# Hybrid decoder step: first output tile and weight splits one or two steps later in the last stage, and the sample's result stored by two transfers

## The chip, the cores and the metric

The kernel runs on one core of a Trainium2 chip. The metric is the device time of one execution in microseconds. Times of engines, waits and transfers come from one profiled execution, whose own clock starts at its first instruction.

## What is computed

One layer of a hybrid trunk, for a prompt of 1024 positions and for 64 sample positions (8 sequences of 8). What the last stage does of it, cut from the reference:

```python
# sample: selected-block attention over a cache of 8192 positions per sequence
s = jnp.einsum('bthgd,bhtkd->bhgtk', q, kb) * SCALE
p = masked_softmax(s, (kpos <= tq[None, None, :, None])[:, :, None])
return jnp.einsum('bhgtk,bhtkd->bthgd', p.astype(vb.dtype), vb)

# prompt and sample: output projection, residual, final norm
def merge(a, z_a, b, z_b, w_out):
    return jnp.concatenate([a * jax.nn.silu(z_a), b * jax.nn.silu(z_b)], axis=-1) @ w_out

x_p = x_p + merge(a_out, z_a, b_out, z_b, w_out[l])   # (1, 1024, 1024)
x_s = x_s + merge(a_out, z_a, b_out, z_b, w_out[l])   # (8, 8, 1024)
return (rmsnorm(x_p, final_g), rmsnorm(x_s, final_g), ...)
```

Arithmetic is float32. The output projection is made of three products of rounded halves: high by high, high by low, low by high.

## The kernel before

Earlier stages do the projections, the prompt's attention and the sample's compressed branch. The last stage, which the change touches, has 64 steps. A step is one piece of the cache (512 positions) of two sequences:

- `load(p_, e)` (line 1590) fetches the step's eight blocks of 128 KB into two `kv` tiles. Most are direct transfers that SP issues, each after a page number that SP loads from `pgt`; the others are gathers that GpSimd (POOL) issues. Up to step 4 one block of eight is a gather, from step 5 on three are. There are twelve `kv` tiles, six steps' worth, so the load of step i+6 needs the tiles of step i, which are free after `o` of step i.
- `step_k` (line 1726) transposes the keys on TensorE (`pk`, eight matmuls), and ACT copies them out (`kt`).
- `step_a` (line 1618) makes the scores (`pss`) and DVE adds the mask and takes the maxima (`Sx`, `st`); `exps` (line 1632) is ACT's exponential over `Sx`, one step later.
- `step_b` (line 1636) transposes the probabilities (`pp` on TensorE, `pT` on ACT); `step_c` (line 1639) multiplies them with the values (`o`), two steps after the scores.

Between these stand the output projection's products (`yacc`): `OutTile` (line 1469) loads a tile of 128 prompt rows (`mt`, one buffer, two transfers), `high` rounds it on ACT (`mh`), `low` makes the remainder on DVE (`ml`), `product` multiplies with the high and low part of `w_out` (`woh`, `wol`). `wo_load` (line 1441) fetches the eight row blocks of `w_out` (`wor`), `wo_split` (line 1451) makes their two parts: the copy is ACT's for odd blocks and DVE's for even ones, the subtraction DVE's. The list `when` gives each product the step from which it is due: the first at step `first`, then evenly up to the last step.

PE, ACT and DVE run in the order in which the loop of line 1745 is written: in step i the exponential of step i-1, the scores of step i, half of the due products around the transposes of step i+1, the transposed probabilities of step i-1, then whatever `at(i, ...)` has listed for this step (tiles' parts first, then weight splits), the other products, and `o` of step i-2. POOL and SP aren't ordered by hand: a scheduler places their transfers. All engines work through their own rows strictly in order.

SP has eight completion semaphores in turn, so that one of its transfers is issued only after the one eight before it has landed.

In the end `SampleTile.finish` (line 1563) normalises the sample's 64 rows, which lie as two halves of 512 columns on 128 partitions (`xf`), and line 1583 stores them. In the names of rows, `kv_9742` and the like are buffer numbers that the build gives; they differ from build to build. SPq is SP's DMA queue, `wor<-in_w_out_dram` a transfer into `wor`.

Of the kernel before, what the change touches and what calls it, by code (L numbers as in the profile page):

```python
# [40 lines left out]
def tok_cols(t):  # L41

    return (0, NS) if t == 0 else (NS + P * (t - 1), P)
# [131 lines left out]
def tile_hymba_gmlp_nsa_decode_step(  # L175
# [9 lines left out]
    V, A, G, TE, SY = (Timed(e, n, clock) for e, n in ((nc.vector, "DVE"), (nc.scalar, "ACT"), (nc.gpsimd, "POOL"),  # L185
                                                       (nc.tensor, "PE"), (nc.sync, "SP")))
# [38 lines left out]
    with ExitStack() as es:  # L225
# [367 lines left out]
        for g_ in ((1, 2, 3, 4, 5, 6, 7, 8), (0,)):  # L593
            for t in g_:
                n = tok_cols(t)[1]
# [12 lines left out]
        for p_ in range(4):  # L608
            for b2 in range(2):
                b = 2 * p_ + b2  # L610
# [110 lines left out]
    with ExitStack() as es:  # L721
# [401 lines left out]
        def prompt_attention():  # L1123
# [197 lines left out]
            for i in range(len(steps) + 1):  # L1321
# [11 lines left out]
                if i >= 2:  # L1333
                    yield done.need_values(1)
                    done.values(1)
                    n_, g_, br_ = steps[i - 2]
                    if g_ in (None, 3):
                        yield [Qs[n_]["o"]] + ([] if g_ is None else [Qs[n_]["x"]]), [] if g_ is None else [tp]
                        collect(Qs[n_], br_)
                    if g_ == 3 and br_ == 1:  # L1340
                        finish(Qs[steps[i - 2][0]])
                        load_z(Qs[steps[i - 2][0] + 1])
# [16 lines left out]
            yield [Qs[7]["o"], Qs[7]["x"]], [tp]  # L1359
            collect(Qs[7], 1)  # L1360
            finish(Qs[7])


# [20 lines left out]
        with tc.manual_schedule(engines={mybir.EngineType.PE, mybir.EngineType.Activation, mybir.EngineType.DVE}):  # L1384
# [5 lines left out]
            while streams or later:  # L1390
# [6 lines left out]
                t = clock.t["PE"]  # L1397
# [8 lines left out]
    with ExitStack() as es:  # L1406
# [27 lines left out]
        def at(step, fn):  # L1434
            todo.setdefault(step, []).append(fn)
# [15 lines left out]
        def wo_split(k):  # L1451
            raw = raws[k]
            if k:
                wol.append(pwo.tile([P, DM], F32R, name="wol", tag="wo", bufs=KC))
            else:
                wol.append(pwo1.tile([P, DM], F32R, name="wol0"))
            (A.copy if k % 2 else V.tensor_copy)(woh[:, k], raw)
            (V if k % 2 else V).tensor_tensor(wol[k], raw, woh[:, k].bitcast(F32), op=ALU.subtract)
# [64 lines left out]
        class SampleTile(OutTile):  # L1523
# [39 lines left out]
            def finish(self):  # L1563
                xt, fg = self.xt, self.fg
                junk = p3b.tile([P, DM], BF16, name="junk", tag="junk", bufs=1)
                ss = p3b.tile([P, 4], F32, name="ss3", tag="ss3")
                rs = p3b.tile([P, 4], F32, name="rs3", tag="ss3")
                for i in range(2):
                    cs = slice(i * 256, i * 256 + 256)
                    V.tensor_tensor(xt[:, cs], xt[:, cs], self.acc[:, cs], op=ALU.add)  # L1570
                    A.activation(junk[:, cs], xt[:, cs], AF.Square, scale=1.0 / 32, accum_out=ss[:, i:i + 1])
                tot = psP.tile([P, 512], F32, name="tot", tag="p")
                for i in range(2):
                    TE.matmul(tot[:, 0:1], both, ss[:, i:i + 1], start=(i == 0), stop=(i == 1))
                G.tensor_tensor(xt, xt, fg, op=ALU.mult)
                V.tensor_scalar(rs[:, 0:1], tot[:, 0:1], EPS, None, op0=ALU.add)
                V.reciprocal(rs[:, 1:2], rs[:, 0:1])
                A.activation(rs[:, 2:3], rs[:, 1:2], AF.Sqrt)

                V.tensor_scalar(rs[:, 1:2], rs[:, 0:1], rs[:, 2:3], rs[:, 2:3], op0=ALU.mult, op1=ALU.mult)  # L1580
                V.tensor_scalar(rs[:, 3:4], rs[:, 1:2], 3.0, rs[:, 2:3], op0=ALU.subtract, op1=ALU.mult)
                V.tensor_scalar(xt, xt, rs[:, 3:4], -0.5, op0=ALU.mult, op1=ALU.mult)
                SY.dma_start(y_sample.rearrange("b t (h c) -> h (b t) c", h=2), xt)


        steps = [(p_, e) for p_ in range(4) for e in range(16)]
# [100 lines left out]
                    V.tensor_tensor(mts[hs, 4:8, ts_], pt_[hs, 0, r_:r_ + 32].rearrange("p (g t) -> p g t", t=TD),  # L1687
                                    zbs[hs, :, ts_], op=ALU.mult)

        n_steps, ahead, first = len(steps), 3, 2  # L1690
        tiles = [OutTile(t) for t in range(1, NT)]
        sample = SampleTile()
        prods = [(o, i) for o in tiles for i in range(6 * KC)]
# [4 lines left out]
        for o, t in zip(tiles, range(len(tiles))):  # L1698
            b0, b1_, b2_ = (when[prods.index((o, i))] for i in (0, 23, 47))
            if t:  # L1700
                at(b0 - 5, o.load)
            at(max(b0 - 3, 0), o.high)
            at(max(b0 - 2, 0), o.low)
            at(b0, o.residual)
            at(b1_ + 1, lambda o=o: o.add(0, o.acc0))
            at(b2_ + 1, lambda o=o: o.add(1, o.acc))
            at(b2_ + 2, o.square)
            at(b2_ + 3, o.root)
            at(b2_ + 4, o.norm)
# [22 lines left out]
        for k in range(KC):  # L1732
            wo_load(k)
        k0 = 0
        for i, n in ((0, 2), (1, 1), (2, 1), (3, 2), (4, 2)):
            for k in range(k0, k0 + n):
                at(i, lambda k=k: wo_split(k))
            k0 += n
# [119 lines left out]
```

## Time and profile before

| | us |
|---|---|
| median of 3 runs (lowest to highest) | 1424.33 (1422.97 to 1429.22) |
| profiled execution, its own time | 1429.88 |
| its span, first to last instruction | 1427.8 |
| the last stage in it, from the first `pk` on | 1061.5 to 1427.8 |

Every row of the profile names an engine, an operation with the tile that it writes and those that it reads, the number of instructions merged into the row, and in brackets the idle time of the engine before it with what ended it. "issue" there is a wait of which the profile shows no cause. The granted clock of TensorE is given as a share of 2.4 GHz (1.00), so 0.50 is 1.2 GHz. The DMA share is the mean of 16 DMA engines, so one engine alone gives 0.06; it can come out a little above 1 when short packets overlap.

### The profile page before, as it was taken

The page shows a single profiled execution, that of the slowest core. Times are in us where ns is not written, and L with a number is a line of the kernel's source. Part 1 is how long each engine was busy: PE and PEld are TensorE (multiplying, and loading weights), DVE is VectorE, ACT ScalarE, POOL GpSimd, SP SyncE. Part 2 cuts the span into 40 slices and gives each one's busy share as a digit, 9 for nine tenths or more (in the row PEclk, how much of TensorE's full clock was granted, in tenths as well). Part 3 has the DMA queues.
Part 4 walks back from the last instruction along what each step waited for, and adds up shares of the span by engine and source line. Part 5 has one row for each costly group of instructions (what it writes and reads, how often), then busy time and mean ns, then how long its engine had stood idle before and what let it go on. Part 6 is the DMA issues. An engine that isn't in the chain of part 4 may idle for free.

```text
span 1427.8 us, 27897 instructions
## 1 busy us (share of the span) xinstructions
PE 1336.1 (94%) x10345; PEld 1044.9 (73%) x10345; DVE 785.2 (55%) x1878; ACT 576.3 (40%) x1275; POOL 568.6 (40%) x684
## 2 busy tenths in 40 slices
PE   6899999999889999999899999999986999999896
PEld 6799999999757776777677776777754666666564
DVE  7527202212487677867678687777765343442334
ACT  5314216421114333354334444263545555555451
POOL 1007426520343363443345343433313566655440
PEclk9999999999999999999999999999998999999998
DMA  7413333535985686665867495663258788787761
GB/s 243 136 36 98 115 80 122 141 65 186 306 298 171 226 302 231 232 207 191 311 223 259 145 320 187 240 224 104 88 183 218 225 254 258 241 249 231 239 193 45
DMA packets 170849, 279.13 MB, mean 196 GB/s; under 512 B 38810, under 2 KB 142234, under 8 KB 154202
## 3 DMA queue, kind: packets, MB, share of 16 engines
q0 software_dynamic: 27168, 158.09, 32.1%
q1 hardware_dynamic: 143546, 119.26, 28.1%
q8 instruction: 82, 1.34, 0.4%
q14 instruction: 53, 0.43, 0.1%
HBM read 252.64 MB, written 24.65 MB: 194 GB/s over the span
## 4 chain that ended last, share of the span: by engine, by line
PE 75%; issue 7%; DVE 7%; DMA 6%; POOL 2%; ACT 1%; SPq 1%; ACTq 0%; DVEq 0%; POOLq 0%
PE acc L125 35%; PE o L125 9%; PE yacc L125 6%; PE pk L125 5%; PE ps L125 5%; PE ppp L125 4%; PE pss L125 4%; DMA R<-in_cache_kv_dram,idx 4%; PE pp L125 2%; PE pv L125 1%; DVE U L125 1%; DVE rs L125 1%; DVE st L125 1%; SPq L125 1%; DVE xn L125 1%
## 5 line engine op out<-in xcount | busy, mean ns | idle before, releaser
L125 PE MATMUL acc<-U,w 128*128 128x256 f32 x1024 | 246.1, 391 | 14.1 <-DVE U L125 14.1
L118 POOL DMA_INDIRECT R<-in_cache_kv_dram,idx x128 | 126.3, 986 | 325.5 <-DVE U L125 264.5
L118 POOL DMA_INDIRECT kv<-in_cache_kv_dram,idx x182 | 180.4, 991 | 174.5 <-PE o L125 72.3
L125 PEld LDWEIGHTS acc<-U,w 128*128 128x128 f32 x1024 | 191.7, 194 | 53.2 <-issue 26.1
L125 DVE STREAM_TRANSPOSE U<-R 128x512 f32<-128x512 f32 x256 | 163.5, 683 | 61.7 <-DMA R<-in_cache_kv_dram,idx 51.5
L125 ACT ACTIVATE Pe<-Pe,st 128x384 f32<-128x384 f32 (+3 forms) x192 | 110.8, 578 | 147.9 <-DVE st L125 147.7
L125 DVE CUSTOM_DVE_ANT_1 Sx<-pss,qsT 128x512 f32<-128x512 f32 x64 | 44.2, 691 | 156.0 <-PE pss L125 122.2
L125 PE MATMUL acc<-EO,ws 128*128 128x256 f32 x512 | 125.3, 393 | 2.2 <-DVE EO L125 2.2
L125 PE MATMUL acc<-xh,wh 128*128 128x362 f32 (+1 forms) x384 | 126.6, 330 | 0.0
L125 PE MATMUL acc<-xl,wh 128*128 128x362 f32 (+1 forms) x384 | 126.0, 328 | 0.0
L125 PE MATMUL acc<-xh,wl 128*128 128x362 f32 (+1 forms) x384 | 126.0, 328 | 0.0
L125 PEld LDWEIGHTS acc<-EO,ws 128*128 128x128 f32 x512 | 95.7, 194 | 25.7 <-issue 13.4
L125 DVE CUSTOM_DVE_ANT_0 Pe<-ps,caus 128x384 f32<-128x384 f32 (+3 forms) x192 | 92.3, 517 | 37.7 <-PE ps L125 33.2
L125 PE MATMUL acc<-wh,xh 128*128 128x256 f32 (+1 forms) x360 | 97.3, 291 | 6.0 <-ACT v_sb L125 4.4
L125 PEld LDWEIGHTS pk<-ident,kv 128*128 128x128 f32 x512 | 55.6, 142 | 59.9 <-issue 43.0
L125 ACT COPY kt<-pk 128x512 f32<-128x512 f32 x128 | 70.2, 587 | 70.0 <-PE pk L125 52.5
L125 PE MATMUL acc<-wl,xh 128*128 128x256 f32 (+1 forms) x360 | 96.0, 288 | 0.0
L125 PE MATMUL ps<-kT,qr 64*128 64x256 f32 (+3 forms) x384 | 85.4, 511 | 4.8 <-DVE pcs L125 3.0
L125 POOL TENSOR_TENSOR EO<-U 128x1024 f32<-128x1024 f32 x32 | 76.9, 2403 | 26.6 <-PE acc L125 24.0
L125 PE MATMUL acc<-wh,xl 128*128 128x256 f32 (+1 forms) x320 | 86.7, 290 | 0.0
L125 PE MATMUL o<-pT,vn 128*64 128x128 f32 x1056 | 81.8, 283 | 3.5 <-DVE pT L125 2.1
L125 DVE TENSOR_TENSOR wl<-wraw,wh 128x1024 fp32r<-128x1024 f32 (+1 forms) x23 | 30.7, 1339 | 97.8 <-ACT wh L125 97.7
(294 smaller groups left out, 2599.2 us busy)
## 6 DMA issues: line engine op xcount, KB each, us to landing
kv<-in_cache_kv_dram SPq DMA_DIRECT2D x330, 128.0 KB
wraw<-in_w_in_dram SPq DMA_DIRECT2D x16, 512.0 KB
wraw<-in_w_in_dram SPq DMA_DIRECT2D x32, 128.0 KB
kvw<-in_state_win_dram SPq DMA_DIRECT2D x8, 512.0 KB
xo<-in_x_prompt_dram SPq DMA_DIRECT2D x8, 512.0 KB
out_dram<-xo SPq DMA_DIRECT2D x8, 512.0 KB
xt<-in_x_prompt_dram SPq DMA_DIRECT2D x7, 512.0 KB
out_dram<-kvw SPq DMA_DIRECT2D x8, 384.0 KB
```

What stands on the lines that cost most here:

```text
L118: return fn(*args, **kw)
L125: return fn(*args, **kw)
```

## The change

```diff
@@ SampleTile.finish
-                SY.dma_start(y_sample.rearrange("b t (h c) -> h (b t) c", h=2), xt)
+                for h in range(2):
+                    SY.dma_start(y_sample.rearrange("b t (h c) -> h (b t) c", h=2)[h], xt[h * 64:h * 64 + 64])
@@ the plan of the last stage
-        n_steps, ahead, first = len(steps), 3, 2
+        n_steps, ahead, first = len(steps), 3, 3
@@
-            at(max(b0 - 3, 0), o.high)
-            at(max(b0 - 2, 0), o.low)
+            at(max(b0 - 3, 2), o.high)
+            at(max(b0 - 2, 2), o.low)
@@
-        for i, n in ((0, 2), (1, 1), (2, 1), (3, 2), (4, 2)):
+        for i, n in ((1, 2), (2, 1), (3, 2), (4, 3)):
             for k in range(k0, k0 + n):
                 at(i, lambda k=k: wo_split(k))
```

Before, the first tile's `high` and `low` and the splits of blocks 0 and 1 stood in step 0, the other splits in steps 1 to 4, and products began in step 2. Now step 0 has none of these, step 1 has the splits of blocks 0 and 1, step 2 has `high`, `low` and block 2, step 3 blocks 3 and 4, step 4 blocks 5 to 7, and products begin in step 3, with 63 instead of 64 steps to spread over. Nothing is computed that wasn't before; one transfer is added.

On ACT at the start of the stage, before (the first two rows are the keys of step 1, `Sx_9887` is step 0's exponential):

```order
L125 COPY kt3_9893<-pk3_9894 128x512
L125 COPY kt3_9900<-pk3_9901 128x512
L125 CAST mh_9907<-mt_9840 128x1024
L125 CAST woh_9734<-wor_9822 128x1024
L125 ACTIVATE Sx_9887,st3_9886<-Sx_9887,st3_9886 128x512
L125 COPY kt3_9950<-pk3_9951 128x512
L125 COPY kt3_9957<-pk3_9958 128x512
L125 COPY pT3_9964<-pp3_9965 128x512
```

and now:

```order
L125 COPY kt3_9893<-pk3_9894 128x512
L125 COPY kt3_9900<-pk3_9901 128x512
L125 ACTIVATE Sx_9887,st3_9886<-Sx_9887,st3_9886 128x512
L125 COPY kt3_9940<-pk3_9941 128x512
L125 COPY kt3_9947<-pk3_9948 128x512
L125 COPY pT3_9954<-pp3_9955 128x512
L125 CAST woh_9734<-wor_9822 128x1024
L125 ACTIVATE Sx_9934,st3_9886<-Sx_9934,st3_9886 128x512
L125 COPY kt3_9999<-pk3_10000 128x512
L125 COPY kt3_10006<-pk3_10007 128x512
L125 COPY pT3_10013<-pp3_10014 128x512
L125 CAST mh_10020<-mt_9840 128x1024
```

Between the keys of step 1 and the cast `mh` there were no rows; now there are nine, the exponentials of steps 0 and 1 among them.

On POOL, whose order follows from the scheduler, the gathers after the small memset before the stage, before (`kv_9931` is step 4's tile, `kv_9977` and `kv_9989` are step 5's, `kv_10056` and `kv_10068` step 6's):

```order
L125 MEMSET zero_9737 128x24
L118 DMA kv_9931<-in_cache_kv_dram,idx3_80 128x256
L118 DMA kv_9977<-in_cache_kv_dram,idx3_80 128x256
L118 DMA kv_9989<-in_cache_kv_dram,idx3_80 128x256 x2
L118 DMA kv_10056<-in_cache_kv_dram,idx3_80 128x256
L118 DMA kv_10068<-in_cache_kv_dram,idx3_80 128x256 x2
```

and now (`kv_9921` is step 4's, `kv_10044` and `kv_10056` are step 6's, `kv_9970` and `kv_9982` step 5's):

```order
L125 MEMSET zero_9737 128x24
L118 DMA kv_9921<-in_cache_kv_dram,idx3_80 128x256
L118 DMA kv_10044<-in_cache_kv_dram,idx3_80 128x256
L118 DMA kv_9970<-in_cache_kv_dram,idx3_80 128x256
L118 DMA kv_9982<-in_cache_kv_dram,idx3_80 128x256 x2
L118 DMA kv_10056<-in_cache_kv_dram,idx3_80 128x256 x2
```

Step 6's first gather, which needs the tile that `o` of step 0 frees, now stands ahead of step 5's three.

On SP after the last direct block of step 5, before:

```order
L125 DMA kv_9989<-in_cache_kv_dram 128x256
L125 DMA mt_10264<-a_scr_61 128x4x128
L125 DMA mt_10264<-b_scr_58 128x4x128
L1598 TENSOR_LOAD pgt_79
L125 ISA
L125 DMA kv_10056<-in_cache_kv_dram 128x256
```

and now:

```order
L125 DMA kv_9982<-in_cache_kv_dram 128x256
L125 ISA
L125 DMA kv_9982<-in_cache_kv_dram 128x256
L1599 TENSOR_LOAD pgt_79
L125 ISA
L125 DMA kv_10044<-in_cache_kv_dram 128x256
```

The second tile's two `mt` transfers, which stood ahead of step 6's blocks, have moved behind step 8's.

## Rows read from the trace of the kernel before

**Rows 1.** The page's first line: the span.

```profile
span 1427.8 us, 27897 instructions
```

**Rows 2.** Busy time by stretches at the start of the last stage: stretch, its length, busy us and instructions of PE, PEld, DVE, ACT, POOL, then the granted clock, the DMA share and GB/s.

```profile
1065.00:1070.00 5.00, 4.33 (x21) 2.17 (x22) 0.85 (x3) 1.40 (x3) 0.00 (x0) 1.00 0.91 256
1070.00:1075.00 5.00, 0.36 (x4) 0.12 (x2) 0.00 (x0) 0.00 (x0) 0.00 (x0) 0.81 1.08 230
1075.00:1080.00 5.00, 0.00 (x0) 0.00 (x0) 1.09 (x1) 2.17 (x3) 0.00 (x0) 0.50 1.04 261
1080.00:1085.00 5.00, 4.41 (x15) 2.47 (x16) 4.80 (x9) 2.94 (x8) 0.00 (x0) 0.50 0.88 260
```

**Rows 3.** TensorE in order of time, 1069 to 1091 us: start, duration, instruction, and in brackets the idle time before it and what ended it.

```profile
1069.26 1.10 PE L125 MATMUL pk<-ident,kv 128*128 128x128 f32 x8
1080.59 1.12 PE L125 MATMUL pp<-ident,Sx 128*128 128x128 f32 x4 [10.24 <-ACT Sx L125]
1081.64 1.98 PE L125 MATMUL pss<-kt,qb 128*64 128x512 f32 x4
1083.55 1.97 PE L125 MATMUL pk<-ident,kv 128*128 128x128 f32 x8
1085.17 0.78 PE L125 MATMUL yacc<-woh,mh 128*128 128x512 f32 x1
...
1086.60 0.67 PE L125 MATMUL pp<-ident,Sx 128*128 128x128 f32 x4
...
1088.48 1.08 PE L125 MATMUL pss<-kt,qb 128*64 128x512 f32 x4
1089.49 1.09 PE L125 MATMUL pk<-ident,kv 128*128 128x128 f32 x8
1090.34 0.48 PE L125 MATMUL yacc<-woh,mh 128*128 128x512 f32 x1
...
1091.12 0.60 PE L125 MATMUL pp<-ident,Sx 128*128 128x128 f32 x4
```

**Rows 4.** ACT in order of time over the same place.

```profile
1067.13 1.07 ACT L125 COPY kt<-pk 128x512 f32<-128x512 f32 x2 [1.81 <-PE pk L125]
1077.83 1.04 ACT L125 CAST mh<-mt 128x1024 fp32r<-128x1024 f32 x1 [9.63 <-DMA mt<-b_scr]
...
1079.73 0.72 ACT L125 ACTIVATE Sx<-Sx,st 128x512 f32<-128x512 f32 x1
```

**Rows 5.** SP's DMA queue in order of time: start of the first issue, time to the end of the last, what is moved, number of transfers.

```profile
1069.86 0.63 SPq L125 DMA_DIRECT2D mt<-b_scr  x1
1071.11 6.12 SPq L125 DMA_DIRECT2D kv<-in_cache_kv_dram  x7
...
1080.56 2.97 SPq L125 DMA_DIRECT2D kv<-in_cache_kv_dram  x5
1083.62 0.54 SPq L125 DMA_DIRECT2D mt<-a_scr  x1
...
1088.58 4.52 SPq L125 DMA_DIRECT2D kv<-in_cache_kv_dram  x5
```

**Rows 6.** The DMA engines' mean busy share in tenths in 40 slices of 0.1 us, from 1077 to 1081 us.

```profile
DMA  9999999989996991112369648999754879999597
```

**Rows 7.** POOL in order of time: one of the four gathers that it issues at the start of the stage, 1.25 us apart, and the next one after them.

```profile
1061.35 0.95 POOL L118 DMA_INDIRECT kv<-in_cache_kv_dram,idx  x1 [0.30 <-issue]
...
1088.82 0.95 POOL L118 DMA_INDIRECT kv<-in_cache_kv_dram,idx  x1 [24.02 <-PE o L125]
```

**Rows 8.** What SP's queue waited for from 1085 to 1115 us (the first two rows) and from 1115 to 1345 us (the largest entry of that answer): us in total, times, longest.

```profile
SPq L125 <- PE o L125: 3.5, 3, 2.9
SPq L125 <- PE pk L125: 1.2, 1, 1.2
...
SPq L125 <- PE o L125: 2.8, 9, 0.4
```

**Rows 9.** The key transposes alone, by stretches of 25 us, with the columns of rows 2 less POOL's; eight on PE are one step.

```profile
1300.00:1325.00 25.00, 5.78 (x40) 4.24 (x40) 0.00 (x0) 5.54 (x10) 1.00 0.73 228
1325.00:1350.00 25.00, 6.05 (x32) 3.51 (x32) 0.00 (x0) 4.58 (x8) 0.93 0.76 240
1350.00:1375.00 25.00, 5.46 (x40) 4.28 (x40) 0.00 (x0) 5.36 (x10) 1.00 0.81 246
```

**Rows 10.** The chain that ended last, the one long transfer in it: start of the issue, time to landing, what.

```profile
1283.22 4.95 DMA kv<-in_cache_kv_dram
```

**Rows 11.** SP's queue near the end of the program: the last load of the sample tile, which has the shape of one half of the result (64 rows of 2 KB), the last prompt tile's store (512 KB) and the sample's (256 KB).

```profile
1391.41 0.60 SPq L125 DMA_DIRECT2D xf<-in_final_g_dram  x1
...
1413.26 0.35 SPq L125 DMA_DIRECT2D out_dram<-xo  x1
1418.57 0.66 SPq L125 DMA_DIRECT2D out_dram<-xf  x1
```

**Rows 12.** Busy time by stretches around these transfers, columns as in rows 2.

```profile
1391.40:1394.00 2.60, 2.36 (x42) 1.45 (x40) 1.02 (x6) 2.08 (x5) 0.00 (x0) 1.00 0.43 127
...
1414.00:1415.50 1.50, 0.87 (x4) 0.38 (x2) 0.59 (x2) 0.09 (x1) 0.00 (x0) 1.00 0.86 350
...
1419.60:1426.10 6.50, 0.00 (x0) 0.00 (x0) 0.00 (x0) 0.00 (x0) 0.00 (x0) 0.50 0.13 42
1426.10:1427.80 1.70, 0.00 (x0) 0.00 (x0) 0.00 (x0) 0.00 (x0) 0.00 (x0) 0.50 0.00 0
```

## The prediction

> **What bounds the kernel now.** I first read the span [rows 1], then busy time by stretches over the start of the last stage [rows 2]. One stretch stands out there: from 1070 to 1080 us TensorE is busy 0.36 of 10 us, while the DMA share is 1.04 to 1.08. TensorE in order of time [rows 3] says for what it stands: the transposes of step 0's probabilities (the first `pp`) wait 10.24 us for `Sx`, which is ACT's exponential. ACT in order of time [rows 4] says why: its row ahead of the exponential is the cast `mh`, which waits 9.63 us for the first tile's `mt`. The scores lay ready; the exponential was stuck behind a cast that nobody on TensorE needed yet. `mt` itself is late since its transfers, issued at 1069.86 [rows 5], share full DMA engines with `w_out` and the cache.
>
> The wait has a tail. The granted clock is 0.50 until TensorE has worked again for some microseconds [rows 2], and the rows there take twice as long [rows 3]: `pp` 1.12 for 0.60 us, `pss` 1.98 for 1.08, `pk` 1.97 for 1.09, and three products from the first's start to the next `pp` 1086.60 - 1085.17 = 1.43 us, later 1091.12 - 1090.34 = 0.78. That is 0.5 + 0.9 + 0.9 + 0.6 = 2.9 us.
>
> Later another thing sets the pace. From 1085 to 1115 us SP's queue waits for TensorE 4.7 us, from 1115 to 1345 us only 2.8 us [rows 8]: there SP, which issues most blocks of the cache, is itself nearly always at work. TensorE meets that from the other side: of 25 us, five steps' worth of `pk`, one stretch has four, at a clock of 0.93 [rows 9]. So one group of late blocks costs a step, 5 us. The chain that ended last passes through such a block, 4.95 us from issue to landing [rows 10].
>
> At the end, the sample's result is issued at 1418.57 and its traffic lasts until 1426.1, at 42 GB/s and a DMA share of 0.13, which is 2 of 16 engines; the span ends 1.7 us later [rows 11, 12]. Nothing lies beside these 6.5 us.
>
> **The change at the start of the stage.** ACT now does step 0's exponential right behind the keys of step 1, at 1067.13 + 1.07 = 1068.2 instead of 1079.73 [rows 4]. `pp` of step 0 is then ready before TensorE wants it, and follows `pk` at 1070.4 instead of 1080.59 [rows 3]. TensorE can go on through the scores, the keys of step 3, the next `pp` and two `o`. Before, from that `pp` to the `o` of step 0 that lets POOL's next gather go [rows 7] it took 1088.8 - 1080.6 = 8.2 us; without the half clock (2.9) and two steps' three products (2 x 0.78 = 1.6) that is 3.7; I take 4.5, as the next transposes may wait for their exponential, so this `o` ends near 1075.
>
> What is late next is the cache. Step 4's blocks are issued until 1071.11 + 6.12 = 1077.2 us [rows 5], and the DMA engines are full until 1078.4 and have brief dips at once after it [rows 6]: the queue has run dry about then. I estimate that step 4's keys are there at 1079.5 and its `pk` ends at 1080.6. Before, it ended at 1089.49 + 1.09 = 1090.6 [rows 3]: 10.0 earlier. Against it stand the products that had been done by then and now are not, these 1.6. That leaves 8.4. The new idle stretch, some 1076 to 1079.5, can bring the half clock back, for nothing up to the 2.9 from above; I take the middle, 1.4, since it is a third as long as the old one. So TensorE allows 7.0, and 8.4 if the clock stays.
>
> The cast `mh` stands in step 2 now, and still waits for `mt`, which lands before 1077.83 [rows 4]. Queued behind it on ACT are the exponential of step 2 and the keys of step 4; ACT gets there about 1076, and TensorE is waiting for step 4's blocks until 1079.5 anyway. That cover is thin: each microsecond of `mt` behind 1078 is one on TensorE.
>
> SP allows less. What the start can give SP is what SP waited for TensorE, 3.5 for `o` and 1.2 for `pk`, 4.7 us [rows 8]; after that it has no waits of size to lose, and it paces the second half. A program that SP paces gains 4.7, one that TensorE paces 7.0 to 8.4. I take **5.5**, near the first, as the missing `pk` in rows 9 speak for SP. The bounds: 8.4 above; below, 4.7 less 2 for POOL, next, so 2.5.
>
> POOL: step 6's first gather moves ahead of step 5's three and waits there for `o` of step 0. Before, gathers went 1.25 us apart at the start [rows 7], without a wait. After, the wait ends near 1075, the three are out at 1075 + 4 x 1.25 = 1080, and down by 1085 if they take the 4.95 of rows 10; step 5's `pk` comes at 1080.6 + 4.9. So I cost it at nothing, but its cover is gone where `o` comes 1 or 2 us late: 0 to 2.
>
> The second tile's `mt` transfers move on SP behind the blocks of step 8: two issues of half a microsecond each [rows 5], done later and not less often. No net. The splits cost the same work; step 4 now has three, some four more rows on DVE at 4.80 / 9 = 0.53 us in the stretch after the wait [rows 2], 2.1 us in a step of 4.9, beside TensorE. First products in step 3 want `ml` from step 2 and block 0's halves from step 1, both earlier in the order. 63 instead of 64 steps for the products moves a product here and there by a step: nothing.
>
> **The change at the end.** Each half is now 64 rows of 2 KB, the shape of the `xf` load of rows 11. That was issued at 1391.41, and the traffic around it lies within 1391.4 to 1394 at 127 GB/s [rows 12], three times the 42 of the store: at most 2.6 us from issue to the last byte. The other neighbour is the prompt tile's store, 512 KB within 1414 to 1415.5 at 350 GB/s, whose traffic starts some 0.8 us after the issue [rows 11, 12]. SP issues the second half about 0.6 after the first. Ends: 1418.57 + 0.6 + 2.6 = 1421.8, or, by the prompt tile, 1418.57 + 0.6 + 0.8 + 0.37 (128 KB at 350 GB/s), with half as much again for the first half, near 1420.6. Before it was 1426.1, so 4.3 to 5.5; I take **5.0**, nearer the store, which goes the same way.
>
> A rule speaks against this part. The Trainium skill, "DMA: Bandwidth & Descriptors", section "Anatomy of one DMA — SWDGE (gpsimd) path", gives each transfer about 2.0 us that do not shrink with size, and the rest at 436 GB/s; it is stated for GpSimd's transfers, and SP issues these. By it 128 KB would be an estimated 2.3 us, two in a row 4.6, the end 1423.2 and the gain 2.9 (the sum 1415.9). The rows speak for the other side: 42 GB/s is two engines' traffic and no fixed time. The same page's section "Why a DMA increments its semaphore by 16 and not by 1" spreads a transfer over the largest count up to 16 that divides its slowest dimension, 2 for the old store and 16 for each half; by that rule the gain comes, and the trace agrees as far as the 0.13 goes.
>
> **Sum.** 5.5 + 5.0 = 10.5. Against the profiled execution: span 1427.8 to 1417.3, its own time 1429.88 to 1419.4. That run is 5.5 us above the median of the three; neither place depends on that, so I take the same 10.5 from the median, 1424.33: **1413.8**. With the bounds 2.5 to 8.4 and 4.3 to 5.5: 1410.4 to 1417.5. A measurement of this kernel can tell about 0.5% (7.1 us) from no change, so faster begins below 1417.2.
>
> **Rivals.**
> *SP eats the start.* If SP paces everything from step 6 on, and POOL's reversed gathers keep step 5 late, the start gives 0 to 2.5 and only the end counts: 1424.3 - 5.0 - (0 to 2.5) = 1416.8 to 1419.3. For it: 2.8 us of waits in 230 [rows 8]. Against: SP did wait 4.7 for TensorE just behind the start. Chance 0.17.
> *The store is no shorter.* If the halves go one after the other, or by few engines each, the end gives at most 1: 1424.3 - 5.5 - 0.5 = 1418.3. Against: the xf load of the same shape. Chance 0.07. (The fixed time of the cited page lies between this and the forecast.)
> *More than forecast.* TensorE's whole 8.4 is kept, and with the cache ahead the late group of rows 9 is missed once more or once less: 8.4 + 5.0 to 8.4 + 5.0 + 5.0, 1410.9 down to 1405.9. Chance 0.09.
> *Slower.* TensorE, 7 us ahead, runs into SP's queue sooner and oftener: each group of late blocks costs a step and brings the half clock with it, 5 us by rows 9. Two more such groups eat the gain; from four it is slower by more than a measurement's grain: 1424.3 - 10.5 + 20 = 1433.8. For it: one already stands in 75 us. Against: SP's pace is its own, and a TensorE that waits for it ends no later than before. Chance 0.05.
>
> **How the numbers follow.** Forecast 0.62. Faster by over 0.5%: forecast and more, 0.62 + 0.09, and a corner of the first rival, 0.02: 0.73. Within: the rest of the first rival and the second, 0.15 + 0.07 = 0.22. Slower 0.05. The range goes from 1408.5 (half of "more") to 1419.5, where the first and second rival end; out of it lie some 0.1, and as the bounds at the start rest on landings that I estimate, I leave it so.
>
> **What would show it.** In the profile after: the first `pp` of the stage follows `pk` without the 10.24; ACT has the exponential at about 1068.2 and `mh` waits there for `mt` by 1 to 3 us, not 9.6; TensorE's next wait is for `kv` of step 4, by some 3 us, and its `pk` ends near 1080.6; the granted clock between 1075 and 1085 is above 0.5. SP's waits for `o` from 1085 on shrink from 3.5 to near nothing. POOL's first gather behind the memset waits until about 1075. At the end two `xf` stores, a DMA share far over 0.13, traffic over 2 to 3 us after the first issue. Wrong would be: step 5's `pk` waiting for gathers, `mh` waiting beyond 1079, stretches like that of rows 9 in greater number, or a last transfer of over 4 us.

## The result

The changed kernel ran in 1416.41 us (median of 9 runs, 1413.36 to 1422.07), the kernel before beside it in 1424.33 (median of 9): ratio 0.9946, 95% interval 0.9928 to 0.9965, so 7.7 us less, 5.0 to 10.3. Forecast were 10.5 less, 1413.8, with 1408.5 to 1419.5 as range. The profiled execution took 1422.07, its span (the page's first line) is

```profile
span 1420.0 us, 27898 instructions
```

7.8 us below [rows 1]. Where they went, in order of time. Busy time by stretches at the start of the stage, columns as in rows 2:

```profile
1065.00:1070.00 5.00, 5.00 (x18) 2.35 (x17) 1.03 (x4) 1.88 (x4) 0.00 (x0) 0.72 1.03 255
1070.00:1075.00 5.00, 4.95 (x61) 3.24 (x61) 4.49 (x9) 4.65 (x9) 0.00 (x0) 1.00 1.10 250
1075.00:1080.00 5.00, 4.65 (x22) 2.45 (x18) 3.54 (x4) 3.33 (x7) 3.95 (x4) 1.00 1.09 288
1080.00:1085.00 5.00, 2.34 (x40) 1.07 (x38) 4.02 (x9) 1.86 (x4) 3.30 (x4) 0.98 0.96 326
1085.00:1090.00 5.00, 4.27 (x15) 3.15 (x16) 0.11 (x1) 1.17 (x2) 2.14 (x3) 0.50 0.77 247
```

The hole of rows 2 between 1070 and 1080 is filled. A smaller one has come behind it, 1080 to 1085, and behind that the granted clock of 0.50. TensorE in order of time, as in rows 3:

```profile
1065.97 1.95 PE L125 MATMUL pk<-ident,kv 128*128 128x128 f32 x8
...
1069.61 1.09 PE L125 MATMUL pk<-ident,kv 128*128 128x128 f32 x8
1070.54 0.60 PE L125 MATMUL pp<-ident,Sx 128*128 128x128 f32 x4
...
1074.21 0.65 PE L125 MATMUL o<-kv,pT 128*32 128x64 f32 x32
...
1075.80 2.65 PE L125 MATMUL pk<-ident,kv 128*128 128x128 f32 x8
...
1084.59 0.73 PE L125 MATMUL pk<-ident,kv 128*128 128x128 f32 x2 [2.66 <-remote]
1085.92 1.93 PE L125 MATMUL pk<-ident,kv 128*128 128x128 f32 x6 [0.60 <-issue]
```

The first `pp` follows `pk` with no wait. `o` of step 0 ends at 1074.86. The `pk` at 1075.80 is step 4's, spread over 2.65 us as its blocks land; step 5's waits 2.66 us and again 0.60. The first row is step 1's `pk`, at half clock (0.53 granted from 1066 to 1067.9 us). It comes 5.64 us behind step 0's instead of the 4.86 of the kernel before, and step 2's 9.27 instead of 7.74. The half clock sets in ahead of the first moved row, and the same kernel in e10 doesn't have it. ACT, as in rows 4, and POOL and SP's queue, as in rows 7 and 5:

```profile
1068.45 0.72 ACT L125 ACTIVATE Sx<-Sx,st 128x512 f32<-128x512 f32 x1
...
1075.35 1.04 ACT L125 CAST mh<-mt 128x1024 fp32r<-128x1024 f32 x1 [0.33 <-DMA mt<-b_scr]
```

```profile
1058.91 0.95 POOL L118 DMA_INDIRECT kv<-in_cache_kv_dram,idx  x1 [29.74 <-ACT pT L125]
1075.13 0.94 POOL L118 DMA_INDIRECT kv<-in_cache_kv_dram,idx  x1 [15.27 <-DMA mt<-b_scr]
...
1079.37 0.96 POOL L118 DMA_INDIRECT kv<-in_cache_kv_dram,idx  x1 [0.30 <-issue]
```

```profile
1069.93 4.80 SPq L125 DMA_DIRECT2D kv<-in_cache_kv_dram  x7
1075.28 0.54 SPq L125 DMA_DIRECT2D zbs<-b_scr  x1
1075.86 0.63 SPq L125 DMA_DIRECT2D mts<-a_scr  x1
1076.59 0.56 SPq L125 DMA_DIRECT2D fgB<-in_final_g_dram  x1
1078.07 17.48 SPq L125 DMA_DIRECT2D kv<-in_cache_kv_dram  x20
```

`mh` waits 0.33 us instead of 9.63. POOL stands at step 6's first gather from 1059.9 to 1075.13; the row names `mt` as what came last, but the start lies 0.3 behind the end of `o` of step 0. Step 5's third gather goes out only at 1079.37. SP issues three small loads ahead of step 5's blocks.

What SP's queue waited for from 1085 to 1115 us, and from 1115 to 1345 us, as in rows 8, then the key transposes by stretches, as in rows 9 (ACT is the last column ahead of the clock):

```profile
SPq L125 <- PE o L125: 2.3, 3, 1.4
SPq L125 <- PE pk L125: 0.2, 1, 0.2
```

```profile
SPq L125 <- PE o L125: 3.3, 10, 0.4
```

```profile
1300.00:1325.00 25.00, 6.57 (x40) 4.23 (x40) 0.00 (x0) 5.63 (x10) 1.00 0.77 243
1325.00:1350.00 25.00, 7.36 (x40) 4.37 (x40) 0.00 (x0) 5.65 (x10) 1.00 0.75 226
1350.00:1375.00 25.00, 6.45 (x38) 4.10 (x38) 0.00 (x0) 5.23 (x9) 1.00 0.77 238
```

The waits for TensorE went from 4.7 to 2.5, not to near nothing. The late group of rows 9 (32 `pk` of 40) is spread here: all stretches have about 40, but they take 6.45 to 7.36 us instead of 5.46 to 6.05.

The end: the stores on SP's queue and busy time by stretches (rows 11 and 12), and what SP's queue waited for, in the changed kernel from 1408 us on, and in the kernel before from 1415 us on:

```profile
1411.99 1.15 SPq L125 DMA_DIRECT2D out_dram<-xf  x2
```

```profile
1413.00:1414.50 1.50, 0.00 (x0) 0.00 (x0) 0.00 (x0) 0.00 (x0) 0.00 (x0) 0.50 0.77 180
1414.50:1420.00 5.50, 0.00 (x0) 0.00 (x0) 0.00 (x0) 0.00 (x0) 0.00 (x0) 0.50 0.00 0
```

```profile
SPq L1855 <- PEq L1855: 4.4, 2, 3.9
SPq L1855 <- DMA out_dram<-xf: 1.4, 2, 0.7
```

```profile
SPq L1854 <- DMA out_dram<-xf: 6.7, 1, 6.7
...
SPq L1854 <- PEq L1854: 0.7, 2, 0.5
```

The transfers do what was forecast: DMA share 0.77 for 0.13, the last byte 2.5 us behind the first issue instead of 7.5. SP waits 1.4 us for them instead of 6.7. But then nothing happens for 5.5 us, and 3.7 of the 5.3 us come back as a wait at the end of the program (4.4 for 0.7; that the view names PE's sequencer is its guess at the releaser). The records of the trace that no view counts as busy name it (start, duration, engine, record; times in us):

```
before   1416.36  9.39  POOL  DRAIN (behind its last operation, xf<-xf, 1416.40 to 1417.66)
         1426.41  0.03  SP    sees the store landed
         1427.01  0.02  POOL  takes all engines' end signals
changed  1409.79  9.39  POOL  DRAIN (behind xf<-xf, 1409.82 to 1411.08)
         1414.28  0.03  SP    sees the first half landed
         1415.00  0.03  SP    sees the second half landed
         1419.22  0.02  POOL  takes all engines' end signals
```

In both, POOL's DRAIN ends 8.1 us behind its last operation. Before, at 1425.75, that was 0.66 ahead of the store's landing and unseen. Now it ends at 1419.18, 4.2 us behind the second landing, and the program ends with it. From the store's first issue to the end of the span it is 8.0 instead of 9.2 us: the store's part gave 1.2.

Since executions differ ahead of the stage and late in it, the start is best read from the first `pk`. Starts of a step's first `pk`, in us behind step 0's (from TensorE in order of time), and the end from the store's first issue, for all kernels; the last column is the ratio with its interval. e1 to e4, e5 to e8 and e9 to e12 ran on one chip each, numbered 4, 2 and 6; the first two rows are the profiles above. The columns of early steps hold different work: by step 8's `pk` the kernel before, e1 and e9 have done 29 products (`yacc`), e7 and e12 18, all others 23, and three products take 0.78 us [rows 3]. At step 63 it is 338 (337 in e7 and e12).

| | `pk` 4 | `pk` 5 | `pk` 8 | `pk` 63 | store to end | ratio |
|---|---|---|---|---|---|---|
| before | 27.97 | 32.80 | 47.89 | 323.97 | 9.21 | 1 |
| changed | 15.47 | 24.25 | 42.84 | 318.57 | 8.00 | 0.9946 (0.9928 to 0.9965) |
| e1, chip 4 | 28.00 | 32.72 | 47.44 | 317.12 | 8.00 | 0.999 (0.9966 to 1.0015) |
| e2, chip 4 | 15.23 | 24.21 | 39.49 | 312.81 | 9.23 | 0.9942 (0.9919 to 0.9964) |
| e3, chip 4 | 15.28 | 23.21 | 39.28 | 314.53 | 4.34 | 0.9917 (0.9889 to 0.9944) |
| e4, chip 4 | 16.03 | 23.77 | 39.82 | 312.91 | 8.00 | 0.9955 (0.9931 to 0.998) |
| e5, chip 2 | 15.32 | 25.21 | 38.35 | 292.51 | 8.00 | 0.997 (0.9943 to 0.9997) |
| e6, chip 2 | 24.20 | 28.66 | 41.80 | 293.88 | 8.00 | 0.9976 (0.9948 to 1.0004) |
| e7, chip 2 | 13.67 | 26.38 | 43.02 | 295.15 | 8.00 | 0.9969 (0.9945 to 0.9993) |
| e8, chip 2 | 15.29 | 23.98 | 38.34 | 296.79 | 4.31 | 0.9922 (0.9897 to 0.9946) |
| e9 (before), chip 6 | 26.46 | 30.93 | 44.06 | 300.36 | 9.25 | 1 |
| e10 (changed), chip 6 | 16.08 | 24.00 | 37.98 | 294.72 | 8.00 | 0.996 (0.9944 to 0.9975) |
| e11, chip 6 | 15.38 | 21.13 | 36.86 | 296.48 | 4.31 | 0.9929 (0.9911 to 0.9948) |
| e12, chip 6 | 13.68 | 22.08 | 39.13 | 293.14 | 4.36 | 0.9936 (0.9915 to 0.9957) |

### The profile page after: what moved, and what is told of

The parts are those of the page before. It is cut to its first block, busy times and chain, and to the rows that moved or that the text cites. A ratio compares the mean times of both kernels' runs of the same rounds, so it can differ in the third digit from the quotient of the medians.

```text
span 1420.0 us, 27898 instructions
## 1 busy us (share of the span) xinstructions
PE 1338.7 (94%) x10345; PEld 1045.5 (74%) x10345; DVE 785.2 (55%) x1878; ACT 576.0 (41%) x1275; POOL 568.1 (40%) x684
## 4 chain that ended last, share of the span: by engine, by line
PE 75%; issue 7%; DVE 7%; DMA 7%; POOL 2%; ACT 1%; SPq 1%; another core or an unknown queue 0%; ACTq 0%; DVEq 0%; POOLq 0%
PE acc L125 35%; PE o L125 8%; PE yacc L125 6%; PE pk L125 5%; PE ps L125 5%; PE ppp L125 4%; DMA R<-in_cache_kv_dram,idx 4%; PE pss L125 4%; PE pp L125 2%; PE pv L125 1%; DVE U L125 1%; DVE st L125 1%; DMA kv<-in_cache_kv_dram 1%; DVE rs L125 1%; SPq L125 1%
## 5 line engine op out<-in xcount | busy, mean ns | idle before, releaser
L125 PE MATMUL acc<-U,w 128*128 128x256 f32 x1024 | 245.4, 390 | 13.5 <-DVE U L125 13.5
L125 PE MATMUL pk<-ident,kv 128*128 128x128 f32 x512 | 78.1, 287 | 7.9 <-remote 2.7
```

The lines of the kernel that those rows point to most:

```text
L125: return fn(*args, **kw)
```

## The experiments

**The two halves of the change.** The kernel before with the two stores, and the changed kernel with the one:

```diff
 e1, from the kernel before
-                SY.dma_start(y_sample.rearrange("b t (h c) -> h (b t) c", h=2), xt)
+                for h in range(2):
+                    SY.dma_start(y_sample.rearrange("b t (h c) -> h (b t) c", h=2)[h], xt[h * 64:h * 64 + 64])
 e2, from the changed kernel: the same lines the other way
```

> The kernel before with the two half stores alone. Theory (POOL): both programs show on POOL a DRAIN of 9.39 us that starts when its last operation on xf starts; before, it ended 0.66 us ahead of the single store's landing, so the store can give at most 1.2 us. From the first issue of the store to the span's end then 8.0 us (9.2 before), ratio 0.998 to 1.000. Rival (the term of the prediction): the end follows the transfers, 5.0 us less, 4.2 from issue to end, ratio 0.9965. In both, the start of the stage is as before: first pp waits about 10 us, first to last pk 324 us.

> The changed kernel with the single store of before. Theory: the start gives what it gave in the changed kernel, first to last pk 318.6 us instead of 324.0, and the end is 9.2 us from the store's issue; so 5.4 us of the whole, ratio 0.9955 to 0.997. Rival (the store gave its 5.0 and the start only 2.7): first to last pk 321 us, ratio 0.998.

e1 has 8.00 us from issue to end, DRAIN 9.39 us again, and a ratio of 0.999, which rules out the prediction's 0.9965 only just (its interval begins at 0.9966); the 8.00 settles it. e2 has 9.23 at the end, and its ratio, 0.9942 where 0.9955 to 0.997 was expected (its interval reaches 0.9964), says that the start alone carries most of the gain. Its last `pk` at 312.8 is also earlier than expected. That is no finding: the kernel before and e1 have the same start, 47.9 and 47.4 at step 8, and yet 324.0 and 317.1 at step 63. One execution says nothing of the late steps below some 7 us.

**POOL out of the end.**

```diff
-                G.tensor_tensor(xt, xt, fg, op=ALU.mult)
+                V.tensor_tensor(xt, xt, fg, op=ALU.mult)
```

> The changed kernel with the sample's multiplication by the norm's weights on DVE instead of POOL, so that POOL's last operation is some 30 us earlier. Theory (POOL's drain holds the end): the drain is over long before, the end follows the second half store, which SP sees landed 3.0 us after the first issue: about 4.5 us from the first issue to the span's end instead of 8.0, DVE adds 0.2, so 3.3 us less than the changed kernel, ratio to before 0.991 to 0.993. Rival (the drain waits for the program's stores or for something at the end, and POOL's operation has no part in it): 8 us remain, ratio 0.9945 to 0.9955.

POOL's last operations are now its casts, the DRAIN ends 8.1 us behind them, at 1379, and the end follows the landing. What SP's queue waited for at the end of e3, and POOL's last row:

```profile
SPq L1855 <- DMA out_dram<-xf: 1.4, 2, 0.7
SPq L1855 <- PEq L1855: 0.7, 2, 0.5
```

```profile
1370.17 0.80 POOL L125 CAST mls<-zero 128x64 fp32r<-128x64 f32 x2
```

From issue to end 4.34 us instead of 8.00, with SP's wait for the transfers still 1.4. So POOL's operation, and not the stores, held the end, and the split does bring its 5 us (9.2 to 4.3) once POOL is out of the way. No run has the single store without POOL's operation; in the kernel before the landing came last already, so little could change by it. The kernel is 0.9917 of before.

**One store from each of two queues**, on top of e3:

```diff
-                    SY.dma_start(y_sample.rearrange("b t (h c) -> h (b t) c", h=2)[h], xt[h * 64:h * 64 + 64])
+                    (nc.scalar if h else SY).dma_start(y_sample.rearrange("b t (h c) -> h (b t) c", h=2)[h], xt[h * 64:h * 64 + 64])
```

> The kernel without POOL's last operation (e3), with the second half store issued by ACT beside SP's. Theory (in e3 the end follows the second store, issued 0.65 us behind the first and seen landed 0.74 behind it): 0.5 to 0.7 us less, 3.7 us from SP's issue to the span's end instead of 4.34. Rival (the transfers share what they wait for, or ACT's queue starts slower): 4.3 or more. The time as e3's within 0.2%, for the size is too small to show in it.

The rival holds: 4.31. Both are issued at 1385.06, and SP sees one landed at 1387.99 and the other at 1388.07, 2.9 and 3.0 us later, where e3's halves were seen 2.3 and 3.0 us behind the first issue. SP's wait in e8:

```profile
SPq L1855 <- DMA out_dram<-xf: 2.3, 1, 2.3
```

**Which moved part freed the exponential.**

```diff
 e5, from the changed kernel: only high and low moved
-        for i, n in ((1, 2), (2, 1), (3, 2), (4, 3)):
+        for i, n in ((0, 2), (1, 1), (2, 1), (3, 2), (4, 2)):
 e6, from the changed kernel: only the splits and the products' first step moved
-            at(max(b0 - 3, 2), o.high)
-            at(max(b0 - 2, 2), o.low)
+            at(max(b0 - 3, 0), o.high)
+            at(max(b0 - 2, 0), o.low)
```

> The changed kernel with the weight splits where they were before (blocks 0 and 1 in step 0, and so on); high and low of the first tile stay in step 2, products begin in step 3. Theory (the exponential was stuck behind mh alone): ACT now has the copy of block 1 of w_out ahead of the exponential of step 0, whose transfers land some 4 us ahead of mt's last; the first pp waits at most 3 us behind pk, and first pk to pk of step 8 is within 1.5 us of the runs with the whole start (39.3 to 42.8). Rival (the splits held it as much as mh): pp waits 5 us or more, and pk of step 8 comes at 45 or later.

> The changed kernel with high and low of the first tile back in step 0, so that only the splits and the products' first step have moved. Theory (mh is what blocks): the first pp waits for Sx some 8 to 10 us as before, first pk to pk of step 8 47 to 48 us, ratio 0.9985 to 1.0. Rival (the splits): pp waits under 4 us, pk of step 8 below 44.

TensorE's first `pp` in e5, and in e6:

```profile
1068.68 0.60 PE L125 MATMUL pp<-ident,Sx 128*128 128x128 f32 x4
```

```profile
1079.60 0.69 PE L125 MATMUL pp<-ident,Sx 128*128 128x128 f32 x2 [7.91 <-ACT Sx L125]
```

e5 has no wait and is at step 8 where e8, the whole start on the same chip, is: 38.35 and 38.34. e6 waits 7.91 us. So moving `high` and `low` alone is enough to free the exponential. e6 came to step 8 at 41.80 instead of the 47 to 48 that I took from another chip's rows; beside e9, whose steps run as fast, it is 2.3 us early. Of that, 0.9 is the first `pp`, 18.2 us behind the first `pk` for 19.0: the cast `woh` of 1.04 us no longer stands between `mh` and the exponential. The rest is that six products come later, 1.6 us that have to be done all the same. Its ratio, expected at 0.9985 to 1.0, lies at 0.9976 with 1.0 in its interval.

**POOL's gathers in their old order.** POOL is added to the engines that follow the code's order, which puts step 5's gathers ahead again:

```diff
-        with tc.manual_schedule(engines={mybir.EngineType.PE, mybir.EngineType.Activation, mybir.EngineType.DVE}):
+        with tc.manual_schedule(engines={mybir.EngineType.PE, mybir.EngineType.Activation, mybir.EngineType.DVE,
+                                         mybir.EngineType.Pool}):
```

> The changed kernel with POOL in the order of the code, which puts step 5's three gathers ahead of step 6's first, as before the change. Theory (the reversed gathers hold step 5): the gathers go out right behind step 4's, by 1065, step 5's pk no longer waits for them but only for SP's blocks, which land by about 1084: the wait of pk of step 5 shrinks from some 5 us by 1.5 to 3, first to last pk 316 to 317.5 us instead of 318.6, ratio 0.9925 to 0.994. Rival (SP's blocks and the full DMA engines set step 5, and earlier gathers only push back step 4's blocks): 0 to 1 us more, first to last pk 318.5 to 319.5.

The theory falls. The gathers went out by 1062.8, and step 5's `pk` waits for nothing; but it starts at 23.77, between the 24.21 of e2 and the 23.21 of e3, which have the reversed order on the same chip. Step 4's came later, 16.03 for 15.23 and 15.28. With the reversed order the waits for step 5 differ from one execution to the next: 3.3 us in the changed kernel's own profile, 1.7 in e3, 0.6 in e8, 0.35 or less in e2 and e10.

**Step 4's blocks ahead of half of w_out**, with everything that needs `w_out` or `mt` one step later, as it would else wait on ACT:

```diff
-        n_steps, ahead, first = len(steps), 3, 3
+        n_steps, ahead, first = len(steps), 3, 4
-            at(max(b0 - 3, 2), o.high)
-            at(max(b0 - 2, 2), o.low)
+            at(max(b0 - 3, 3), o.high)
+            at(max(b0 - 2, 3), o.low)
-        for i in range(ahead):
+        for i in range(5):
-        for i, n in ((1, 2), (2, 1), (3, 2), (4, 3)):
+        for i, n in ((2, 2), (3, 2), (4, 2), (5, 2)):
-                if i + ahead < n_steps:
+                if 5 <= i + ahead < n_steps:
```

> The changed kernel with step 4's seven direct blocks issued ahead of four of w_out's transfers and of mt, and everything that needs w_out or mt one step later (high and low in step 3, splits from step 2, products from step 4). Theory (the order of SP's queue decides: after the change step 4's pk waits for its blocks, which stand behind 4 MB): they land some 3 us earlier, pk of step 4 no longer waits, first pk to pk of step 4 about 14.3 us instead of 15.2 to 16.0 at its start and without the gaps inside it, pk of step 8 at 37 to 39, 1 to 3 us less than the other runs. Rival (the DMA engines are full, and the same bytes have to pass before step 6 whatever their order): pk of step 4 is early, but pk of step 5 and 6 wait as much more, pk of step 8 at 39 to 43, no gain.

Step 4 comes at 13.67 and runs through, then step 5 waits 9.5 us:

```profile
1086.74 1.92 PE L125 MATMUL pk<-ident,kv 128*128 128x128 f32 x5 [9.50 <-DMA kv<-in_cache_kv_dram]
```

Step 8 is 4.7 us behind e5's and e8's, with five products fewer done. The bytes have only changed places, as the rival had it. In the whole time the loss doesn't show clear of noise: 0.9969, where e5 has 0.997.

**Neighbours on one chip, and the small loads.** e9 and e10 are the kernels before and after, unchanged. e11 is e8, e12 is e8 with e7's edit, both with

```diff
-        at(1, lambda: SY.dma_start(zbs, b_scr[:, :, 0:NS]))
-        at(1, lambda: SY.dma_start(mts[:, 0:4, :], a_scr[:, :, 0:NS]))
-        at(1, lambda: SY.dma_start(fgB, final_g.rearrange("(o d) -> o d", o=1).to_broadcast([P, DM])))
+        at(4, ...)                                     # the same three
```

> The kernel before, unchanged, on the chip of this call, so that the rows of the others have a neighbour from the same chip (the two calls so far came to chips on which the last stage takes 313 to 319 and 293 to 297 us). Expected by every theory: the first pp 19 us behind the first pk and waiting about 10 for Sx, 9.2 us from the store's issue to the end.

> The changed kernel, unchanged. Theory: against e9 first pk to pk of step 8 is 4 to 8 us less, the end 8.0 us after the store's issue, and ratio 0.994 to 0.997 (start 3 to 6.5 us, store 1.2). Rival (the gain at the start is given back by later waits for the cache where the chip runs the steps faster): ratio above 0.998.

> e8 (no POOL operation at the end, two queues for the store) with the loads of zbs, mts and fgB, 768 KB in all, moved on SP from ahead of step 5's blocks to behind step 7's. Theory (after the change the full DMA engines between 1062 and 1085 set the start): step 5's blocks come some 2 to 3 us earlier, pk of step 5 at 21 to 22.5 us behind the first pk instead of 23.2 to 25.2, ratio 0.989 to 0.992. Rival (step 4's blocks are the wait, step 5's follow at PE's pace): pk of step 5 as before at 23 to 25, ratio as e8's 0.992.

> e11 with step 4's blocks ahead of four of w_out's transfers and everything that needs those one step later, as in e7, where pk of step 5 then waited 9.5 us for its blocks behind w_out, mt and the three small loads. Theory (the small loads' place cost e7 its gain): pk of step 4 at 13.7 us, of step 5 at 20 to 23, of step 8 at least 1 us ahead of e11's, ratio 0.987 to 0.991. Rival (bytes only change places): step 5 waits 5 us or more again, pk of step 8 is behind e11's, ratio 0.992 or more.

The first `pp` of e9, then TensorE and ACT at this place in e10:

```profile
1075.24 1.12 PE L125 MATMUL pp<-ident,Sx 128*128 128x128 f32 x4 [10.21 <-ACT Sx L125]
```

```profile
1067.66 0.60 PE L125 MATMUL pp<-ident,Sx 128*128 128x128 f32 x4
...
1071.33 0.65 PE L125 MATMUL o<-kv,pT 128*32 128x64 f32 x32
...
1075.06 1.81 PE L125 MATMUL pk<-ident,kv 128*128 128x128 f32 x5 [2.07 <-DMA kv<-in_cache_kv_dram]
1077.23 0.87 PE L125 MATMUL pk<-ident,kv 128*128 128x128 f32 x3 [0.36 <-DMA kv<-in_cache_kv_dram]
...
1079.18 1.05 PE L125 MATMUL pp<-ident,Sx 128*128 128x128 f32 x4
...
1082.98 0.79 PE L125 MATMUL pk<-ident,kv 128*128 128x128 f32 x4
1084.12 0.80 PE L125 MATMUL pk<-ident,kv 128*128 128x128 f32 x4 [0.35 <-DMA kv<-in_cache_kv_dram]
```

```profile
1065.56 0.73 ACT L125 ACTIVATE Sx<-Sx,st 128x512 f32<-128x512 f32 x1
...
1074.63 1.04 ACT L125 CAST mh<-mt 128x1024 fp32r<-128x1024 f32 x1 [2.49 <-DMA mt<-b_scr]
```

The pair gives the start 6.1 us at step 8, of which 1.6 are six products not yet done, 5.6 at step 63, and the store 1.25. In e10 the 10.2 us have become 2.4 us of waits for step 4's blocks, and the `pp` behind them takes 1.05 instead of 0.60: the granted clock fell once more. In e11 step 5 does come 2.9 us earlier (21.13 for 24.00), as its theory had it, step 8 still 1.1 earlier, and in the whole it is lost, as the rival had it: 0.9929, where e3 and e8 have 0.9917 and 0.9922 without it. In e12 step 5 waits 5.18 us again:

```profile
1080.43 0.45 PE L125 MATMUL pk<-ident,kv 128*128 128x128 f32 x1 [5.18 <-DMA kv<-in_cache_kv_dram]
```

## Why the prediction was right, and where not

**The start: the mechanism holds, and the size with some luck.** 5.5 us were forecast, 2.5 to 8.4 (the lower bound, 4.7 less 2, should have been 2.7, which moves the range by 0.2). At step 63, where as many products are done, e9 and e10 show 5.6 and the first two profiles 5.4; the whole time less the store's 1.2 gives 6.5 (the result's ratio) and 4.4 (e10's). At step 8 it is 6.1 and 5.0, or 4.5 and 3.5 without the 1.6 of products not yet done, which the prediction had counted. Step by step, in us behind the first `pk`:

| | forecast (from 1061.5) | changed | e10 |
|---|---|---|---|
| step 0's exponential | 6.7 | 8.1 | 6.6 |
| first `pp` | 8.9 | 10.2 | 8.7 |
| `o` of step 0 over | 13.5 | 14.5 | 13.0 |
| step 4's `pk` over | 19.1 | 18.1 | 19.1 |

e10 has the order and the times of the forecast. In the changed kernel's profile the half clock at steps 1 and 2 came first. Its absolute times (the exponential at 1068.45 for 1068.2, `pp` at 1070.54 for 1070.4, `o` over at 1074.86 for 1075) agree by luck, since its stage also began 1.2 us earlier; by step 4, whose blocks TensorE waited for, the delay was gone. What was late next was step 4's cache, as said. The half clock that I charged with 1.4 us came back behind that wait in e10, and behind step 5's in the changed kernel's profile. e5 and e6 show that `high` and `low` are the part of the change that counts. `mh` waits 0.33 us in one execution and 2.49 in e10 (1 to 3 forecast), under the wait for step 4.

**POOL's reversed gathers cost nothing that shows,** the value taken: e4, without them, has step 5 between e2 and e3, which have them.

**SP as the pace-setter was argued, not shown.** SP's waits for TensorE behind the start fell from 4.7 to 2.5 us and not to near nothing, so only by 2.2, while the start gave 4.4 to 6.5, more than these waits gave up. The 5.5, chosen between 4.7 and TensorE's 7.0 to 8.4, came out well without its reason being borne out. The late groups are still there, in other places. Whether they give back a part of the start on a faster chip, the runs can't say: from step 12 to step 63 one execution differs from another of like start by several us.

**The end: the step that failed is "Nothing lies beside these 6.5 us".** The term was 5.0, bounds 4.3 to 5.5; it measured 1.2. The transfers themselves came as priced: the last byte 2.5 us behind the first issue, forecast 2.0 to 3.2. What lay beside them was POOL's DRAIN, over 0.66 us ahead of the old store's landing. No busy row shows it; the row that should have made me ask is the span's end in rows 12, 1.7 us behind the last byte, which I carried over as a constant. e3 takes the cover away and the 5 us appear: 9.2 to 4.3. With this term right, the sum would have been 5.5 + 1.2 = 6.7, 1417.6, beside the measured 1416.4. That the time still fell within the stated range is the width of the range: it reached up to 1419.5 for rivals, of which "The store is no shorter" (chance 0.07) had the size of the end, at most 1, for another reason.

The estimate from the Trainium skill, "DMA: Bandwidth & Descriptors", section "Anatomy of one DMA — SWDGE (gpsimd) path", stated for GpSimd's transfers, of 2.3 us for each half agrees with the trace of SP's: 2.3 and 2.4 us from issue until SP saw it landed (1411.99 to 1414.28, 1412.61 to 1415.00). Taken in a row, 4.6, it doesn't: they overlap but for the issue, 3.0 in all. The rule of the Trainium skill on the same page, section "Why a DMA increments its semaphore by 16 and not by 1", which gives 16 engines for 64 rows, agrees as far as a share of 0.77 goes, 12 of 16 engines in the mean.

## What to carry to other kernels

Before a last transfer is made shorter, list what every engine does until its last record, records included that count as no work (a drain, a barrier); what ends next is the bound of the gain. An engine that works in order should meet its inputs in the order in which they land: a cast for a late transfer belongs behind the work that is ready. And where the DMA engines are full, a wait that is removed comes back as the wait for the next bytes, so the gain is priced from when those land; to change the order of the same bytes moves the wait only.

The best version here is e3, the change with the last multiplication on DVE: 0.9917 of the kernel before (0.9889 to 0.9944), and e8, the same with two queues, 0.9922; the intervals don't tell them apart.

## What the runs showed of the hardware

POOL's DRAIN at the program's end lasted until 8.1 us behind POOL's last operation (8.09 to 8.10) in all fourteen profiles of this document, whether that was a multiplication at 1410 us, as in the changed kernel, or a cast at 1371 with the stores 34 us away, as in e3. What it does in these 8.1 us no run shows.

Chips differ for the same program: on chip 4 and in the first two profiles the stage takes 313 to 324 us from the first `pk` to the last step's, on chips 2 and 6 293 to 300. The difference sits in one operation: `o`, 32 small matmuls, from 1100 to 1340 us in the changed kernel, in the kernel before, and in e5 on chip 2 (count, busy us, mean ns, then idle before them):

```profile
L125 PE MATMUL o<-kv,pT 128*32 128x64 f32 x1536 | 43.9, 223 | 10.0 <-issue 8.3
```

```profile
L125 PE MATMUL o<-kv,pT 128*32 128x64 f32 x1536 | 43.7, 223 | 9.2 <-issue 7.7
```

```profile
L125 PE MATMUL o<-kv,pT 128*32 128x64 f32 x1667 | 34.3, 222 | 0.0
```

The single matmul takes 222 to 223 ns on either, but on the slower chip they follow each other less closely: 1536 of them keep TensorE busy for 43.9 us, where at e5's rate it would be 31.6, and there are 10.0 us of idle time besides, 8.3 of them with no cause shown. So times are compared within one chip's runs only, and a stage's rows with rows of the same chip.

The granted clock can differ between executions of one kernel at the same place. Step 1's `pk` took 1.95 us at a granted clock of 0.53 in the changed kernel's profile and 1.10 at 1.00 in e10, with the same idle times of 0.28 and 1.47 us on TensorE ahead of it. Five of the fourteen profiles have the lower level there: the changed kernel's and, at 0.50, e3, e5, e6 and e11.
